# Two-layer hybrid encoder: attention bias made during the preceding feed-forward, layer norm vectors fetched later, eps added on VectorE, softmax normalising and transposes ordered later

## The chip, the cores and the metric

The kernel runs on one core of a Trainium2 chip. The metric is the device time of one execution in microseconds. The engines go by their names in the profile: PE is TensorE (PEld its weight loads), DVE is VectorE, ACT is ScalarE, POOL is GpSimd, SP is SyncE, which here issues every DMA of the kernel.

## The reference

An encoder of two layers over 256 tokens of 1024 features. Each layer is a feed-forward, three token mixers side by side, and a second feed-forward, each followed by a layer norm:

```python
for l in range(DEPTH):
    x = layer_norm(ALPHA * x + 0.5 * swiglu(x, ffn1_w_gate[l], ffn1_w_up[l], ffn1_w_down[l]), ln_g[l, 0], ln_b[l, 0])
    proj = x @ w_in[l]
    u, gb, gc, h, q, k, v = jnp.split(proj, splits, axis=-1)
    y_a = pool_mixer(u, pool_w[l], pool_scale[l])
    y_b = gated_conv_mixer(gb, gc, h, conv_w[l])
    y_c = neighbourhood_attention(q, k, v, rpb[l])
    y = jnp.concatenate([y_a, y_b, y_c], axis=-1) @ w_out[l]
    x = layer_norm(ALPHA * x + y, ln_g[l, 1], ln_b[l, 1])
    x = layer_norm(ALPHA * x + 0.5 * swiglu(x, ffn2_w_gate[l], ffn2_w_up[l], ffn2_w_down[l]), ln_g[l, 2], ln_b[l, 2])
```

`layer_norm` is `(x - mu) * rsqrt(var + eps) * g + b`; `swiglu` is `(silu(x @ w_gate) * (x @ w_up)) @ w_down` with an inner width of 2816. The attention has 8 heads of 64 features on a grid of 4 rows and 64 columns: a query sees 16 columns of all 4 rows, a learned bias that depends on the distance in rows and columns is added to its scores, scores outside its columns are set to -1e30, and a softmax follows.

## The kernel before

**Products and weights.** All 256 tokens stay on chip as two tiles of 128 (`t` = 0, 1), and all weights pass through once, in units of 512 KB. Products are to be exact in float32, so each weight unit is split into two parts: SP fetches it into `raw` (L183), ACT copies it to `whi`, rounded (L178), DVE subtracts that from `raw` into `wlo` (L179). Each activation is split the same way (`xhi`, `xlo`; L270 and L271), and each product is three matmuls: hi by hi, lo by hi, hi by lo. They stand in three helpers: `x_stat` (L290 to L292, one token tile against 512 columns), `w_stat` (L303 to L305, 128 columns against all tokens) and `r_stat` (L315 to L317, down and out projections). There are 4 `raw` buffers, so SP can be four units ahead of the splits, and 24 buffers for `whi` and `wlo`, so up to 12 units can be split and not yet used up.

**Order of the work.** Every engine runs its instructions in the order in which the code writes them. A `Pacer` sets it: each group of matmuls advances a clock of estimated TensorE time, `pc.at(delay, tag, fn)` writes a piece of work at the first step that is `delay` us later on this clock, `pc.need(tag)` writes it at once, and each step writes the load and split of one more unit, so long as no more than 12 are alive. The delays are constants at the top of the file. They place an instruction between others and hold nothing back at run time; there an instruction waits for its operands and for its buffers.

**Layer norm.** At the end of each part `finish` does the last products, and for each token tile `ln_stats` (L333, L334) and `ln_rest`: mean and variance are gathered (bn_aggr, L341), POOL adds eps (L342) and takes the power of -1/2 (L343) into `rs`, DVE subtracts the mean and multiplies by `lng` (L345, two halves), then multiplies by `rs` and adds `lnb` (L347, two halves). `transpose_x` then makes `xhi` and `xlo` of the next part: PE transposes (L268), ACT and DVE split (L270, L271). The vectors `lng` and `lnb` are copied to all 128 partitions by two DMAs of 512 KB each (`load_gb`, L325 and L326); `GB_AT` sets how long after the end of a part those of the next are fetched.

**Mixers.** For each token tile the projections `v` and `u` with one gate come first (`x_stat`); the second result is copied to `un` by ACT (L639) and transposed by PE (L644), and from it POOL makes the pooling mixer's means (L602 to L614), to which the pooling product (L619) belongs. Then `w_stat` makes q0, k0, q1, k1, and the two parts of the convolution mixer; the out projection and `finish` end the part.

**Attention.** Four heads are done after k0 (`q` = 0) and four after k1 (`q` = 1), in stages that are hooks of the Pacer: scores on PE (L686), bias added by DVE into `Sb` (L695), maximum (L697), exp on ACT into `pz` with its sum `sm` (L700); `A_NORM` later the normalising on DVE (reciprocal L710, multiplication L712); `A_TR` after that four transposes for each head on PE (L721), copied by ACT (L726, `PT`); `A_PV` after that the product with v (L735), split into `yT` by ACT and DVE (L748, L749).

**Bias.** `load_bias` (L568) fetches the bias of four heads by four DMAs on SP (L572) into `rbias`, and two additions on POOL (L579) put the mask on it, into `bias`. `rbias` and `bias` have one buffer each. For q = 0 this is written at the beginning of the mixers, which in POOL's order comes between the two powers of the layer norm and the means; for q = 1 it is written after the scores of q = 0.

**Feed-forward.** `ffn` does the first 512 of the 2816 columns with the token tiles apart (DVE's `hf`, L396, is transposed by PE, L408), then 9 pairs of 256 columns each for gate and up (`w_stat`), with the down projection (`r_stat`) of an earlier pair behind each; its loop is `for p in range(2, NPAIR)`.

Of the kernel before, what the change touches and what calls it, by code (L numbers as in the profile page):

```python
# [12 lines left out]
ALU = mybir.AluOpType  # L13
# [18 lines left out]
EPS = 1e-5  # L32
# [13 lines left out]

# units of the weights that go before the second token tile at the start, and where its transposes stand
X1_AT = 4
X1_TR = 3
# how long after its operands were ordered a step is issued, in microseconds of the tensor engine's work  # L50
LN_TR = (4.5, 7.2)
GB_AT = 14.0
H_TR = 4.1
# [3 lines left out]
A_STEP = 0.8  # L57
A_NORM = 2.6
A_TR = 1.2
A_PV = 1.4  # L60
# about how long a product of the tensor engine takes: these pace the work of the other engines
MM512 = 0.218
# [3 lines left out]
class Pacer:  # L66
    """Places work of the other engines, and the next weights, between groups of matrix products."""

# [52 lines left out]
def encoder_kernel(  # L121
# [34 lines left out]
    def mirrored(v):  # L156
        """The same view, its last axis run backwards."""
        dims = [list(d) for d in v.ap]
        step, n = dims[-1]
        dims[-1] = [-step, n]  # L160
        return bass.AP(tensor=v.tensor, offset=v.offset + (n - 1) * step, ap=dims)
# [7 lines left out]

# [1 line left out]
    def unit_tiles(shape):  # L171
# [33 lines left out]
    def behind(p):  # L205
        """The pairs whose down projection follows pair p's gate and up projections."""
        return [q for q in ([0, 1] if p == 2 else [p - 1]) if q < NPAIR - TAIL]
# [32 lines left out]

# [1 line left out]
    xs = [xp.tile([P, D], F32, tag=f"x{t}", name=nm("x")) for t in range(NT)]  # L242
# [29 lines left out]

# [1 line left out]
    def x_stat(ps, key, cols, t, xT, free):  # L274
        """One token tile against columns of the weights, a step per unit."""
        k = 1024 // cols
        ts = slice(t * P, (t + 1) * P)
        for i in range(KC // k):
            x_stat_unit(ps, key, i, cols, ts, xT)
            if free:  # L280
                pc.free((*key, i))
            if i < KC // k - 1:
                pc.step(3 * k * MM512)
# [10 lines left out]
    def w_stat(ps, key, xT):  # L294
        """256 columns of the weights against all tokens, transposed out."""
        for ft in range(2):
            c = slice(ft * P, (ft + 1) * P)
            for i in range(2):
                hi, lo = pc.get((*key, i))
                for j in range(4):  # L300
                    kc = i * 4 + j
                    o = ps[:, ft * SEQ : (ft + 1) * SEQ]
                    PE.matmul(o, hi[:, j, c], xT[0][:, kc, :], start=(kc == 0), stop=False)  # L303
                    PE.matmul(o, hi[:, j, c], xT[1][:, kc, :], start=False, stop=False)  # L304
                    PE.matmul(o, lo[:, j, c], xT[0][:, kc, :], start=False, stop=(kc == KC - 1))  # L305
                if ft == 1:
                    pc.free((*key, i))
                if ft == 0 or i == 0:
                    pc.step(12 * MM256)

    def r_stat(ps, key, act, t, n, first, last):
        """A chunk of transposed activations against half a row unit."""
        hi, lo = pc.get(key)
        ts = slice(t * P, (t + 1) * P)
        PE.matmul(ps, act[0][:, ts], hi[:, n, :], start=first, stop=False)  # L315
        PE.matmul(ps, act[1][:, ts], hi[:, n, :], start=False, stop=False)  # L316
        PE.matmul(ps, act[0][:, ts], lo[:, n, :], start=False, stop=last)  # L317

# [1 line left out]
    gbs = []  # L320
# [15 lines left out]
    def ln_rest(t, stats, store):  # L336
        g, b = gbs[-1]
        xt = xs[t]
        mv = sp.tile([P, 2], F32, tag="mv", name=nm("mv"))
        rs = sp.tile([P, 1], F32, tag="rs", name=nm("rs"))  # L340
        DVE.bn_aggr(mv, stats.rearrange("p a b -> p (a b)"))  # L341
        POOL.tensor_scalar(rs, mv[:, 1:2], EPS, None, ALU.add)  # L342
        POOL.tensor_tensor(rs, rs, half_t, ALU.pow)  # L343
        for h in range(2):
            DVE.scalar_tensor_tensor(xt[:, hs[h]], xt[:, hs[h]], mv[:, 0:1], g[:, hs[h]], ALU.subtract, ALU.mult)  # L345
        for c in hs:
            DVE.scalar_tensor_tensor(xt[:, c], xt[:, c], rs[:, 0:1], b[:, c], ALU.mult, ALU.add)  # L347
            if store:
                SP.dma_start(out[0, t * P : (t + 1) * P, c], xt[:, c])

    def finish(keys, act, acc, last_key, next_gb, store, stop):
        """The last products into acc, one token tile after the other, and the layer norm."""
        nT = None if store else new_xT()
        for t in range(NT):
            stats = sp.tile([P, 2, 6], F32, tag="stats", name=nm("stats"))
            # the first half of the columns is done early where something waits for the layer norm
            by_half = t == 0 or store
# [26 lines left out]

# [1 line left out]
    def new_h():  # L386
# [12 lines left out]
    def ffn(key, xT, next_gb, stop, store=False):  # L399
# [16 lines left out]

        # first four column tiles with the token tiles apart
        gk, uk = (*key, "g", 0), (*key, "u", 0)
# [42 lines left out]
        def act(k):  # L461
            f = k[-1]
            return [hts[f // 2][:, i, f % 2, :] for i in range(2)]

        for p in range(2, NPAIR):
            gate = bank()
            w_stat(gate, (*key, "g", p), xT)
            sg = silu(gate)
            pc.step(12 * MM256)
            up = bank()  # L470
            w_stat(up, (*key, "u", p), xT)
            hT = hts[p] = new_h()
            hf = gated(up, sg).rearrange("p (a b) -> p a b", a=2)
            ACT.copy(hT[:, 0], hf)  # L474
            DVE.tensor_tensor(hT[:, 1], hf, f32(hT[:, 0]), ALU.subtract)
            pc.step(12 * MM256)
            pc.need("h")
            # the down projection runs behind
            for q in behind(p):
                for f in (2 * q, 2 * q + 1):  # L480
                    k = (*key, "d", f)
                    for t in range(NT):
                        for n in range(2):
                            if acc[t][n] is None:
                                acc[t][n] = bank("acc")
                            r_stat(acc[t][n], k, act(k), t, n, f == 0, False)
                        if t == 1:
                            pc.free(k)
                        pc.step(6 * MM512)
        keys = [(*key, "d", f) for f in range(2 * (NPAIR - TAIL), NCH)]  # L490
        return finish(keys, act, acc, keys[-1], next_gb, store, stop)

# [1 line left out]
    consts = {}  # L494

    def setup():
        icnt = cp.tile([P, 2, SEQ], F32, tag="icnt", name="icnt")
        for g, w in enumerate(WINDOWS):
# [3 lines left out]
            for t in list(range(w // 2)) + list(range(SEQ - w // 2 + 1, SEQ)):  # L502
                cnt = min(t - w // 2 + w, SEQ) - max(t - w // 2, 0)
                POOL.memset(icnt[ps_ : ps_ + 64, j, t : t + 1], 1.0 / cnt)
        # additive mask of a query column block: its rows run with the column falling
        mask = cp.tile([P, 2, KW], F32, tag="mask", name="mask")
        POOL.memset(mask, 0.0)
        half = NA_COLS // 2
        for r in range(ROWS):
            for b in range(2):  # L510
                m = mask[r * QB : (r + 1) * QB, b, :]
                # key column minus query column is k + q + off
                off = b * KOFF - b * QB - (QB - 1)
# [30 lines left out]
        pc.at(30, "cw", columns)  # L544
        # the bias table, each line in the middle of a longer one
        tab = ap_.tile([P, 7 * TABW], F32, tag="a", name="tab")
# [7 lines left out]
        for r in range(ROWS):  # L554
            dt_ = tc.dram_tile([DEPTH * HEADS, ROWS, TABW], F32, name=f"tab{r}")
            pc.at(20 + 2 * r, "tab", lambda r=r, dt_=dt_: SP.dma_start(dt_, tabv[:, ROWS - 1 - r : 2 * ROWS - 1 - r, :]))
            tabs.append(dt_)
        # probabilities: the columns out of a block's reach stay zero
        pz = []
# [6 lines left out]

# [1 line left out]
    def load_bias(l, q):  # L568
        n = 4 * ROWS
        rv = bp.tile([P, n, WIN], F32, tag="rbias", name=nm("rbias"))  # L570
        for r in range(ROWS):
            SP.dma_start(  # L572
                rv[r * QB : (r + 1) * QB, :, :],
                dram(consts["tabs"][r], (l * HEADS + 4 * q) * ROWS * TABW, [[1, QB], [TABW, n], [1, WIN]]),
            )
        bias = bp.tile([P, 2, n, KW], F32, tag="bias", name=nm("bias"))
        for b in range(2):
# [4 lines left out]
            )  # L582
        return bias

    def mixers(l, xT, next_gb, stop):
# [11 lines left out]
        POOL.memset(U[:, :, PADL + SEQ :], 0.0)  # L597
        biases = {0: load_bias(l, 0)}

# [70 lines left out]
        def attention(j, qT, kT, q):  # L670
            """Two heads, in the upper and the lower half of the rows: one stage after the other."""
            st = {}
# [97 lines left out]
        qk(0)  # L770
        pc.at(A_S + A_STEP + 2, "bias1", lambda: biases.update({1: load_bias(l, 1)}))
        qk(1)
# [73 lines left out]
```

## Time and profile before

| | |
|---|---|
| runs before | 979.34, 980.66, 981.9 us; median 980.66 |
| span of the profiled execution (no other time is given for it) | 979.4 us |
| mean granted clock of TensorE | 0.991 |
| mixers of layer 0 and of layer 1, about | 198 to 296 us, 678 to 780 us |

The page cuts the span into 40 slices of 24.5 us. PE is below nine tenths busy in the first slice, in the tenth (220 to 245 us, in the mixers of layer 0), in the 29th and 30th (686 to 735, in those of layer 1), and in the last:

```profile
PE   7999999998999999999999999999889999999996
POOL 4000000024101000000000000002050000000001
PEclk9999999999999999999999999999989999999999
```

Each digit is the busy share of a slice in tenths; PEclk is the clock granted to PE, in tenths of full speed. POOL works at the start, where it makes constants, and in the mixers.

A row of a timeline is the start and the length in us, engine, line, operation and result<-operands, and in brackets the idle time ahead of it with what ended it. A row of the waits is who waited for what, with us in total, times, and the longest. SPq is the queue in which SP issues DMAs; its rows are the issue, not the transfer.

### The profile page before, as it was taken

Reading aid. Unit: us, or ns where it says so; the run is one execution under the profiler, and the core shown is the slowest. Engines: PE = TensorE matmul, PEld = TensorE weight load, DVE = VectorE, ACT = ScalarE, POOL = GpSimd, SP = SyncE. Lnnn points to the kernel's source line nnn. Section 1 sums busy time; section 2 is a strip of 40 time slices with the busy share of each in tenths; the row PEclk is TensorE's granted clock in tenths of the full one; section 3 lists DMA queues with packets and bytes.
Section 4 is the critical chain, followed back from the end, with each engine's and each line's share of the span. In section 5 each row is a group of like instructions: output and inputs, shape, how many; then the busy total and the mean of one; then the engine's idle time right before and its main releaser. Section 6 shows DMA issues by size and latency. Waiting matters only on the chain.

```text
span 979.4 us, 15259 instructions
## 1 busy us (share of the span) xinstructions
PE 950.6 (97%) x6201; PEld 865.1 (88%) x6201; DVE 580.3 (59%) x670; ACT 437.7 (45%) x585; POOL 65.6 (7%) x118
## 2 busy tenths in 40 slices
PE   7999999998999999999999999999889999999996
PEld 5999999878888999999888999998688889999995
DVE  5755544676768644545676454548676776454525
ACT  6544434335734534434344444443465354344410
POOL 4000000024101000000000000002050000000001
PEclk9999999999999999999999999999989999999999
DMA  8887665568345866565468556664754377556601
GB/s 287 277 264 216 190 194 173 145 185 241 106 129 169 258 194 188 175 195 177 135 211 254 176 172 194 191 186 110 252 153 123 109 229 243 177 174 193 192 23 43
DMA packets 129077, 178.95 MB, mean 183 GB/s; under 512 B 14752, under 2 KB 100848, under 8 KB 129008
## 3 DMA queue, kind: packets, MB, share of 16 engines
q1 hardware_dynamic: 129008, 177.99, 59.3%
q8 instruction: 48, 0.79, 0.3%
q14 instruction: 21, 0.17, 0.0%
HBM read 176.84 MB, written 1.13 MB: 182 GB/s over the span
## 4 chain that ended last, share of the span: by engine, by line
PE 83%; DVE 7%; DMA 5%; issue 2%; ACT 1%; POOL 1%; SPq 1%; POOLq 0%; DVEq 0%; ACTq 0%
PE mm L303 16%; PE mm L304 16%; PE mm L305 16%; PE acc L315 9%; PE acc L316 9%; PE acc L317 9%; DMA raw<-in_w_in_dram 3%; DVE wlo L179 2%; PE mm L292 2%; PE mm L290 2%; PE mm L291 2%; ACT whi L178 1%; PE mm L721 1%; DMA raw<-in_ffn_w_down_dram 1%; DMA raw<-in_ffn_w_up_dram 1%
## 5 line engine op out<-in xcount | busy, mean ns | idle before, releaser
L179 DVE TENSOR_TENSOR wlo<-raw,whi 128x1024 fp32r<-128x1024 f32 (+1 forms) x321 | 390.0, 1231 | 303.1 <-ACT whi L178 302.0
L178 ACT CAST whi<-raw 128x1024 fp32r<-128x1024 f32 (+1 forms) x321 | 331.1, 1045 | 328.9 <-issue 131.2
L303 PE MATMUL mm<-xhi,whi 128*128 128x256 f32 x1344 | 384.0, 286 | 0.0
L304 PE MATMUL mm<-xlo,whi 128*128 128x256 f32 x1344 | 382.0, 284 | 0.0
L305 PE MATMUL mm<-xhi,wlo 128*128 128x256 f32 x1344 | 381.8, 284 | 0.0
L303 PEld LDWEIGHTS mm<-xhi,whi 128*128 128x128 f32 x1344 | 259.7, 193 | 3.0 <-issue 1.5
L304 PEld LDWEIGHTS mm<-xlo,whi 128*128 128x128 f32 x1344 | 259.6, 193 | 1.4
L305 PEld LDWEIGHTS mm<-xhi,wlo 128*128 128x128 f32 x1344 | 259.5, 193 | 0.0
L315 PE MATMUL acc<-whi,hT 128*128 128x512 f32 x352 | 137.9, 392 | 0.0
L316 PE MATMUL acc<-whi,hT 128*128 128x512 f32 x352 | 137.4, 390 | 0.0
L317 PE MATMUL acc<-wlo,hT 128*128 128x512 f32 x352 | 137.0, 389 | 0.0
L317 PEld LDWEIGHTS acc<-wlo,hT 128*128 128x128 f32 x352 | 66.1, 188 | 14.0
L291 PE MATMUL mm<-whi,xlo 128*128 128x512 f32 x192 | 75.3, 392 | 2.9 <-DVE xlo L271 2.9
L315 PEld LDWEIGHTS acc<-whi,hT 128*128 128x128 f32 x352 | 66.2, 188 | 12.7
L316 PEld LDWEIGHTS acc<-whi,hT 128*128 128x128 f32 x352 | 66.2, 188 | 12.3
L290 PE MATMUL mm<-whi,xhi 128*128 128x512 f32 x192 | 76.7, 399 | 0.4 <-ACT whi L178 0.4
L292 PE MATMUL mm<-wlo,xhi 128*128 128x512 f32 x192 | 75.2, 392 | 0.5 <-DVE wlo L179 0.5
L342 POOL TENSOR_SCALAR rs<-mv 128x1 f32<-128x1 f32 x12 | 9.4, 780 | 847.0 <-DVE mv L341 847.0
L474 ACT CAST hT<-hf 128x512 fp32r<-128x512 f32 x36 | 22.3, 620 | 75.2 <-DVE hf L396 75.2
L291 PEld LDWEIGHTS mm<-whi,xlo 128*128 128x128 f32 x192 | 36.4, 189 | 10.8 <-DVE xlo L271 3.8
L292 PEld LDWEIGHTS mm<-wlo,xhi 128*128 128x128 f32 x192 | 36.2, 188 | 8.9 <-DVE wlo L179 1.3
L290 PEld LDWEIGHTS mm<-whi,xhi 128*128 128x128 f32 x192 | 36.3, 189 | 8.2 <-ACT whi L178 1.3
(93 smaller groups left out, 556.9 us busy)
## 6 DMA issues: line engine op xcount, KB each, us to landing
raw<-in_ffn_w_up_dram SPq DMA_DIRECT2D x88, 512.0 KB, 4.7
raw<-in_ffn_w_down_dram SPq DMA_DIRECT2D x88, 512.0 KB, 4.1
raw<-in_ffn_w_gate_dram SPq DMA_DIRECT2D x87, 512.0 KB, 4.1
raw<-in_w_in_dram SPq DMA_DIRECT2D x40, 512.0 KB, 4.7
raw<-in_w_out_dram SPq DMA_DIRECT2D x16, 512.0 KB, 4.8
lng<-in_ln_g_dram SPq DMA_DIRECT2D x6, 512.0 KB, 6.8
lnb<-in_ln_b_dram SPq DMA_DIRECT2D x6, 512.0 KB, 8.3
rbias<-tab SPq DMA_DIRECT2D x16, 96.0 KB, 5.1
```

Of the source, the lines that this page charges most:

```text
L178: ACT.copy(hi, raw)
L179: DVE.tensor_tensor(lo, raw, f32(hi), ALU.subtract)
L290: PE.matmul(ps, xT[0][:, kc, ts], hi[:, j, :], start=(kc == 0), stop=False)
L291: PE.matmul(ps, xT[1][:, kc, ts], hi[:, j, :], start=False, stop=False)
L292: PE.matmul(ps, xT[0][:, kc, ts], lo[:, j, :], start=False, stop=(kc == KC - 1))
L303: PE.matmul(o, hi[:, j, c], xT[0][:, kc, :], start=(kc == 0), stop=False)
L304: PE.matmul(o, hi[:, j, c], xT[1][:, kc, :], start=False, stop=False)
L305: PE.matmul(o, lo[:, j, c], xT[0][:, kc, :], start=False, stop=(kc == KC - 1))
L315: PE.matmul(ps, act[0][:, ts], hi[:, n, :], start=first, stop=False)
L316: PE.matmul(ps, act[1][:, ts], hi[:, n, :], start=False, stop=False)
L317: PE.matmul(ps, act[0][:, ts], lo[:, n, :], start=False, stop=last)
L474: ACT.copy(hT[:, 0], hf)
```

## The change

Five things change. The eps addition goes from POOL to DVE (new L343). `GB_AT` goes from 14 to 45. `A_NORM` goes from 2.6 to 3.6 and `A_TR` from 1.2 to 2.2, so that the normalising is written 1 us later on the Pacer's clock, and the transposes and the products with v 2 us later. `load_bias` is cut into `fetch_bias` (the DMAs, new L579) and `add_mask` (the additions, new L590): for q = 0 both, and for q = 1 the fetch, are written in the first feed-forward of the layer, at the pair p = 6. The additions for q = 1 stay in the mixers, 1 us later on the clock than before. Comments and docstrings go too. Line numbers rise by 1 up to about line 462 and by 7 to 13 behind it: L721 becomes L734, L712 becomes L725.

```diff
@@
-GB_AT = 14.0
+GB_AT = 45.0
...
-A_NORM = 2.6
-A_TR = 1.2
+A_NORM = 3.6
+A_TR = 2.2
 A_PV = 1.4
+BIAS_AT = A_S + A_STEP + 3.0
@@ ln_rest
         DVE.bn_aggr(mv, stats.rearrange("p a b -> p (a b)"))
-        POOL.tensor_scalar(rs, mv[:, 1:2], EPS, None, ALU.add)
+        DVE.tensor_scalar(rs, mv[:, 1:2], EPS, None, ALU.add)
         POOL.tensor_tensor(rs, rs, half_t, ALU.pow)
@@ ffn
+        def bias_ahead():
+            ahead["bias"] = {0: add_mask(fetch_bias(key[0], 0))}
+            ahead["rv"] = fetch_bias(key[0], 1)
+
         for p in range(2, NPAIR):
+            if key[1] == 0 and p == 6:
+                pc.at(0, "bias", bias_ahead)
@@
-    def load_bias(l, q):
+    def fetch_bias(l, q):
         n = 4 * ROWS
         rv = bp.tile([P, n, WIN], F32, tag="rbias", name=nm("rbias"))
...
+        return rv
+
+    def add_mask(rv):
+        n = 4 * ROWS
         bias = bp.tile([P, 2, n, KW], F32, tag="bias", name=nm("bias"))
...
         return bias
 
+    ahead = {}
+
@@ mixers
-        biases = {0: load_bias(l, 0)}
+        biases, rv1 = dict(ahead.pop("bias")), ahead.pop("rv")
...
         qk(0)
-        pc.at(A_S + A_STEP + 2, "bias1", lambda: biases.update({1: load_bias(l, 1)}))
+        pc.at(BIAS_AT, "bias1", lambda: biases.update({1: add_mask(rv1)}))
         qk(1)
```

SP's order in the mixers of layer 0, before: the layer norm vectors stand among the weights of the k0 and q1 projections (`in_w_in_dram`).

```order
L183 DMA raw_2206<-in_w_in_dram 128x4x256
L183 DMA raw_2218<-in_w_in_dram 128x4x256
L325 DMA lng_2230<-in_ln_g_dram 128x1024
L326 DMA lnb_2231<-in_ln_b_dram 128x1024
L183 DMA raw_2234<-in_w_in_dram 128x4x256
L183 DMA raw_2247<-in_w_in_dram 128x4x256
L183 DMA raw_2260<-in_w_in_dram 128x4x256
```

SP's order at pair 6 of the first feed-forward now, where before the two down units were followed directly by the two gate units:

```order
L184 DMA raw_1183<-in_ffn_w_down_dram 128x1024
L184 DMA raw_1201<-in_ffn_w_down_dram 128x1024
L579 DMA rbias_1220<-tab_588 32x16x48
L579 DMA rbias_1220<-tab_589 32x16x48
L579 DMA rbias_1220<-tab_590 32x16x48
L579 DMA rbias_1220<-tab_591 32x16x48
L579 DMA rbias_1228<-tab_588 32x16x48
L579 DMA rbias_1228<-tab_589 32x16x48
L579 DMA rbias_1228<-tab_590 32x16x48
L579 DMA rbias_1228<-tab_591 32x16x48
L184 DMA raw_1257<-in_ffn_w_gate_dram 128x4x256
L184 DMA raw_1277<-in_ffn_w_gate_dram 128x4x256
```

The eight bias fetches moved here from the mixers; the second four write the buffer that the first four filled. In the mixers, SP's rows around the layer norm vectors are now these, behind the last units of the out projection:

```order
L184 DMA raw_2649<-in_w_out_dram 128x1024
L184 DMA raw_2688<-in_w_out_dram 128x1024
L326 DMA lng_2771<-in_ln_g_dram 128x1024
L327 DMA lnb_2772<-in_ln_b_dram 128x1024
L184 DMA raw_2775<-in_ffn_w_gate_dram 128x2x512
L184 DMA raw_2807<-in_ffn_w_gate_dram 128x2x512
```

The vectors moved past 14 weight units.

DVE's order in the attention of layer 0, q = 0, from the last maximum on, before:

```order
L695 TENSOR_TENSOR Sb_2499<-acc_2487,bias_2098 128x320
L697 TENSOR_REDUCE mx_2501<-Sb_2499 128x2
L710 RECIPROCAL sm_2476<-sm_2476 128x2
L712 TENSOR_SCALAR pz_592<-pz_592,sm_2476 128x4x40 x2
L710 RECIPROCAL sm_2483<-sm_2483 128x2
L712 TENSOR_SCALAR pz_594<-pz_594,sm_2483 128x4x40 x2
```

And now:

```order
L708 TENSOR_TENSOR Sb_2500<-acc_2488,bias_1225 128x320
L710 TENSOR_REDUCE mx_2502<-Sb_2500 128x2
L180 TENSOR_TENSOR wlo_2533<-raw_2531,whi_2532 128x1024
L723 RECIPROCAL sm_2477<-sm_2477 128x2
L725 TENSOR_SCALAR pz_592<-pz_592,sm_2477 128x4x40 x2
L723 RECIPROCAL sm_2484<-sm_2484 128x2
L725 TENSOR_SCALAR pz_594<-pz_594,sm_2484 128x4x40 x2
```

A split of a weight (`wlo`) moved ahead of the normalising.

PE's order around the transposes of the same heads, before (between the projections q1, `mm_2453`, and k1, `mm_2607`):

```order
L303 MATMUL mm_2453<-xhi_1960,whi_2219 128x256
L304 MATMUL mm_2453<-xlo_1961,whi_2219 128x256
L305 MATMUL mm_2453<-xhi_1960,wlo_2220 128x256
L721 MATMUL mm_2573<-ident,pz_592 128x128 x4
L721 MATMUL mm_2580<-ident,pz_594 128x128 x4
L721 MATMUL mm_2587<-ident,pz_596 128x128 x4
L721 MATMUL mm_2594<-ident,pz_598 128x128 x4
```

And now (`mm_2572` is the projection k1, `pT` the pooling mixer's means):

```order
L304 MATMUL mm_2572<-xhi_1973,whi_2249 128x256
L305 MATMUL mm_2572<-xlo_1974,whi_2249 128x256
L306 MATMUL mm_2572<-xhi_1973,wlo_2250 128x256
L632 MATMUL mm_2600<-pT_2332,pw 128x256 x2
L734 MATMUL mm_2609<-ident,pz_592 128x128 x4
L734 MATMUL mm_2616<-ident,pz_594 128x128 x4
L734 MATMUL mm_2623<-ident,pz_596 128x128 x4
L734 MATMUL mm_2630<-ident,pz_598 128x128 x4
L304 MATMUL mm_2572<-xhi_1973,whi_2236 128x256
```

The transposes moved 24 matmuls on, into the middle of k1, and behind the pooling product, which stood behind the product with v before.

## Prediction

> **What bounds the kernel now.** I read the page's share of each engine first, then TensorE's waits, then, at the lines named there, the windows, the timelines and the chain.
>
> ```profile
> PE 950.6 (97%) x6201; PEld 865.1 (88%) x6201; DVE 580.3 (59%) x670; ACT 437.7 (45%) x585; POOL 65.6 (7%) x118
> ...
> 95.00:178.00 83.00, 83.00 (x608) 79.17 (x608) 42.89 (x40) 35.79 (x41) 0.00 (x0) 1.00 0.61 181
> ```
> The second row is a window of steady feed-forward (length; busy time of PE, PEld, DVE, ACT, POOL; granted clock; DMA share; GB/s): PE is busy for all of its 83.00 us, so nothing of the change can gain there. All that can go is in what PE waits for:
>
> ```profile
> PE mm L644 <- ACT un L639: 6.2, 2, 3.2
> PE mm L268 <- DMA x<-in_x_dram: 4.8, 2, 3.6
> PE mm L721 <- DVE pz L712: 4.6, 4, 1.4
> PE mm L291 <- DVE xlo L271: 2.9, 2, 1.5
> PE mm L408 <- DVE hf L396: 1.1, 2, 0.9
> ```
> (us in total, times, longest.) L268 is the load of x at the start, which the change leaves alone. The other four come in pairs or fours, once or twice per layer: 14.8 us.
>
> **Layer norm in front of the mixers (L291), gain 2.9.**
>
> ```profile
> 192.71 1.42 DVE L347 SCALAR_TENSOR_TENSOR x<-x,rs,lnb 128x512 f32<-128x512 f32 x2 [0.46 <-POOL rs L343]
> ...
> 202.43 4.10 DVE L347 SCALAR_TENSOR_TENSOR x<-x,rs,lnb 128x512 f32<-128x512 f32 x2 [0.47 <-POOL rs L343]
> ...
> 202.46 3.52 POOL L579 TENSOR_TENSOR bias<-rbias,mask 128x640 f32<-128x640 f32 x2
> ...
> 209.65 0.39 PE L292 MATMUL mm<-wlo,xhi 128*128 128x512 f32 x1
> 209.88 0.39 PE L290 MATMUL mm<-whi,xhi 128*128 128x512 f32 x1
> 211.73 0.50 PE L291 MATMUL mm<-whi,xlo 128*128 128x512 f32 x1 [1.47 <-DVE xlo L271]
> ```
> The same pair of L347 takes 1.42 us for the first token tile and 4.10 for the second, where the two bias additions run on POOL: 2.68 longer. The Trainium skill ("SBUF — State Buffer", SBUF: two separate sides) calls the port that VectorE and GpSimd share an exclusive lock, held for a whole instruction; the 4.10 against 1.42 agrees. In the changed kernel no addition stands there, so DVE comes to xlo some 2.7 us earlier, and PE's 1.47 us of waiting ends, in both layers: 2.9. Behind a wait PE also restarts slowly: from 209.88 to 211.73 are 1.85, of which 1.47 is wait and 0.23 one product (209.65 to 209.88); 0.15 is left, which goes with each wait.
>
> **Fetch of the layer norm vectors (L644 and L408), gain 9.0 and 1.1.**
>
> ```profile
> 209.80 0.42 SPq L326 DMA_DIRECT2D lnb<-in_ln_b_dram  x1
> ...
> 210.32 9.67 DMA raw<-in_w_in_dram
> ...
> raw<-in_w_in_dram SPq DMA_DIRECT2D x40, 512.0 KB, 4.7
> ...
> 227.76 1.11 PE L644 MATMUL mm<-ident,un 128*128 128x128 f32 x4 [3.17 <-ACT un L639]
> ...
> 498.47 9.60 DMA raw<-in_ffn_w_down_dram
> ```
> The chain runs through a weight transfer of 9.67 us, issued at 210.32, right behind lnb (and lng ahead of it, 0.5 MB each), where the median of its kind is 4.7: some 5 late, and the split of that weight (and un behind it on ACT) is late at PE, which stands 3.17 at L644. At the start of the next feed-forward the chain has the same (9.60), and L408 stands. Moved to 45 us, lng and lnb fall behind the weights of the out projection, into stretches where weights wait for free buffers (rows of SP below). Removed: 6.2 and 1.1. The long wait costs the clock too:
>
> ```profile
> 223.00:228.50 5.50, 2.33 (x17) 2.12 (x16) 4.56 (x4) 3.89 (x5) 0.00 (x0) 0.90 0.86 267
> 228.50:231.00 2.50, 2.50 (x14) 2.50 (x13) 1.56 (x2) 1.06 (x2) 1.30 (x1) 0.53 0.83 293
> ```
> Around and behind it the granted clock is 0.90 and 0.53: PE's busy time there is longer by 2.33 x 0.10 + 2.50 x 0.47 = 1.4, in both layers 2.8. So 6.2 + 2.8 = 9.0. Unknown is the new price of lng and lnb: from nothing, if weights are far enough ahead, to the two 3.17 us and their clock again, if they aren't; I take nothing, since these places have no wait of PE in the steady row.
>
> **Attention, net gain 2.9.** Before, the normalising (L712) is in DVE's order right behind the maxima, and PE's transposes (L721) wait for it (rows of DVE, POOL, ACT and PE in layer 0, one timeline after the other):
>
> ```profile
> 246.71 2.67 DVE L712 TENSOR_SCALAR pz<-pz,sm 128x160 f32<-128x160 f32 x2
> 249.30 0.15 DVE L710 RECIPROCAL sm<-sm 128x2 f32<-128x2 f32 x1
> 249.48 0.52 DVE L712 TENSOR_SCALAR pz<-pz,sm 128x160 f32<-128x160 f32 x2
> ...
> 251.16 1.22 DVE L179 TENSOR_TENSOR wlo<-raw,whi 128x1024 fp32r<-128x1024 f32 x1
> ...
> 246.16 3.05 POOL L579 TENSOR_TENSOR bias<-rbias,mask 128x640 f32<-128x640 f32 x2 [5.45 <-DVE Sb L695]
> ...
> 248.53 1.03 ACT L178 CAST whi<-raw 128x1024 fp32r<-128x1024 f32 x1
> ...
> 247.96 0.30 PE L721 MATMUL mm<-ident,pz 128*128 128x128 f32 x1 [0.87 <-DVE pz L712]
> ...
> 251.60 0.36 PE L303 MATMUL mm<-xhi,whi 128*128 128x256 f32 x1
> ...
> 254.64 1.95 PE L735 MATMUL mm<-PT,v 128*64 128x256 f32 x16
> 256.52 1.13 PE L619 MATMUL mm<-pT,pw 128*128 128x256 f32 x4
> ...
> 267.58 2.55 PE L721 MATMUL mm<-ident,pz 128*128 128x128 f32 x16
> ```
> The first normalising takes 2.67 beside POOL's second additions instead of 0.52. These begin when the last Sb has been read, and no table moves that. But the order puts a split (wlo) ahead of the normalising now, and it waits for whi, which ACT makes behind the eight exps: 248.53 + 1.03 = 249.56. Then wlo 1.22, the reciprocal and the first pair of L712 (0.15 + 0.52): the first pz is there at about 251.5. POOL is done by 249.2, so its cover is gone. PE was ready at 247.96 - 0.87 = 247.1. Ahead of the transposes it has now the 24 products that stood behind them (251.60 to 254.64: 3.0) and the pooling product (at most 1.13): ready between 250.1 and 251.2. It waits 0.3 to 1.4; I take 1.0, where layer 0 waited 2.0 (11.00 less 8.95 in the window below). In the second half, which had no wait (267.58), the same 24 products bring PE to 270.6, and whi, wlo and the first pair follow the exps:
>
> ```profile
> 267.90 1.03 ACT L178 CAST whi<-raw 128x1024 fp32r<-128x1024 f32 x1
> ```
> 267.90 + 1.03 + 1.22 + 0.67 = 270.8, and the weighted products of the first half and their yT now stand right ahead of these scores on DVE, some 0.9 (an estimate: a wlo of 1.22 less what it overlaps), so 271.7: a wait of about 1.2. New: 2 x (1.0 + 1.2) = 4.4, about as much as goes (4.6); I count the two as even. Its bounds are 0 and, if whi comes late in each, 2 x 3.2.
>
> What goes besides is clock. The three windows are attention in layer 0, and twice in layer 1:
>
> ```profile
> 241.00:252.00 11.00, 8.95 (x74) 7.76 (x73) 10.72 (x23) 8.41 (x27) 3.13 (x4) 1.00 0.40 134
> ...
> 722.00:734.00 12.00, 9.43 (x66) 8.89 (x65) 10.71 (x22) 8.28 (x26) 3.57 (x5) 0.80 0.32 100
> 734.00:737.50 3.50, 3.50 (x24) 3.37 (x23) 1.23 (x1) 1.12 (x2) 0.00 (x0) 0.71 0.55 153
> ```
> Two microseconds idle in 11 left the clock at 1.00; 2.6 in 12 took it to 0.80 and 0.71: 9.43 x 0.20 + 3.50 x 0.29 = 2.9. With about 1.0 in each stretch I expect no drop: gain 2.9.
>
> **Cost at nothing, with its cover.** In the feed-forward ahead of the mixers SP now issues four small transfers, and four more that need the same single buffer:
>
> ```profile
> 178.42 2.06 SPq L572 DMA_DIRECT2D rbias<-tab  x4
> ...
> DMA to landing us min/median/max: 4.6/5.1/6.3
> ...
> L579 POOL TENSOR_TENSOR bias<-rbias,mask x8: 1540/1550/2013, 202.5 to 728.3; 128x640 f32<-128x640 f32 x8
> ...
> SPq L183 <- DVE wlo L179: 71.1, 29, 4.0
> ```
> The second four wait until both additions have read the first: 2.06 + 5.1 + 2 x 1.55 + 2.06 = 12.3 us in which no weight is asked for. In the steady window SP waits 71.1 of 83 us for a free buffer, 29 times: a unit lasts 83 / 29 = 2.9 us, four are landed or in flight and up to 12 split, so I put the reserve at 30 us and the cost at nothing; without the reserve it is 12.3 per layer. The additions can hold up one wlo there by 3.1 us, inside the same reserve. The two transfers of lng and lnb are in the same position.
>
> The eps addition leaves POOL for DVE, six layer norms with two tiles each. DVE has no such row; the nearest is its reciprocal of a column pair, 0.15 (above), and the other end is nothing, since DVE idles 0.46 ahead of L347 anyway.
>
> ```profile
> 200.60 0.78 POOL L342 TENSOR_SCALAR rs<-mv 128x1 f32<-128x1 f32 x1 [7.92 <-DVE mv L341]
> ```
> 0.78 becomes some 0.15 to 0.2, so L347 waits little or no more; it counts at the end of the program alone, where nothing covers it: 0.3. Elsewhere it is hidden by the products of the next stage.
>
> **The sum**, against the profiled span of 979.4: 2.9 (L291) + 9.0 (L644 with its clock) + 2.9 (attention's clock, its waits even) + 1.1 (L408) + 0.3 (end) + 4 x 0.15 = 0.6 (restarts of the two L291 and two L408) = 16.8, so 962.6. The page gives no other time for that execution; the runs' median of 980.66 is 1.3 above the span, which I add: **963.9 us**. If the two least certain terms, attention's new waits and the clock behind them, miss by 3 either way, it is 961 to 967.
>
> **The rivals.**
> 1. *Attention's new waits cost the clock.* The first wait stands behind whi, so it can be 2 or 3 instead of 1. For it: 2.6 us in two pieces was enough in layer 1. Against: 2.0 was not, in layer 0. Price: 2.9 in each layer, where the sum has none: 963.9 + 5.8 = 969.7. By the Trainium skill ("TensorE: Matmul & The Clock Gate", What's actually happening) the clock halves after an idle window of about 3.4 us, which runs freely; by that, waits near 1 would cost nothing, and the 0.80 after 2.6 in pieces shows that less is enough.
> 2. *The waits vanish*, because whi is earlier on ACT with L644 undelayed: 963.9 - 4.4 = 959.5. Against it: whi stands behind the exps in the order.
> 3. *L644 stays.* It is the ring of four raw buffers that makes weights late there, not lng and lnb: 963.9 + 9.0 = 972.9. Against it: 9.67 against a median of 4.7.
> 4. *Slower: the 12.3 us of SP starve PE* in both first feed-forwards, with a drop of the clock behind each (1.2 as 2.50 x 0.47): 963.9 + 2 x 13.5 = 990.9. It decides where fewer than five units (12.3 / 2.9) are in reserve; SP's 71.1 us of waiting for buffers speak against it.
> 5. *The change doesn't do what it says:* the time of POOL's additions comes back beside other DVE work and all waits find new causes: 980.7.
>
> **How the numbers follow.** Chances: forecast 0.51, rival 1 0.20, rival 2 0.12, rival 3 0.10, rival 4 0.04, rival 5 0.03. The range takes the forecast's own, rival 2 with 3 below it, and rival 1 with 2 above: 956.5 to 971.5; rivals 3 to 5 (0.17) are left out. Faster by over 0.3% (what a measurement of this kernel can tell from no change) is all but rivals 4 and 5: 0.93; within 0.3%: 0.03; slower: 0.04.
>
> **What would show it.** Right: L644, L291 and L408 gone from PE's waits; L347 at 1.42 in both tiles; no raw transfer near 9.6 in the mixers; L734 (the transposes' new line) with four waits of about 1; clock 1.00 in both layers' mixers. Wrong: a wait of PE on whi or wlo in a first feed-forward (rival 4), L644 in the list (rival 3), a clock under 0.9 behind the transposes (rival 1). The weakest step is the 1.0 and 1.2 of attention, which rest on ACT's order and not on a row.

## The result and the profile after

The changed kernel takes 966.28 us (median of 4 runs, 964.41 to 966.65), the kernel before in the same comparison 981.28 (979.34 to 982.71): a ratio of 0.9848, with a 95% interval of 0.9832 to 0.9865. The gain is 15.0 us where 16.8 was forecast. The profiled execution has a span of 964.9 against 979.4. The page and then TensorE's waits of the changed kernel:

```profile
PE 946.9 (98%) x6201; PEld 861.3 (89%) x6201; DVE 572.1 (59%) x682; ACT 437.4 (45%) x585; POOL 58.6 (6%) x106
...
PE   7999999998999999999999999999999999999996
```

```profile
PE mm L269 <- DMA x<-in_x_dram: 4.9, 2, 3.5
PE mm L657 <- ACT un L652: 3.4, 2, 2.5
PE mm L734 <- DVE pz L725: 1.4, 4, 0.6
PE mm L409 <- DVE hf L397: 0.3, 1, 0.3
```

L269 is the start, which stayed. L291's wait on xlo (L292 now) has left the list. L657 is the old L644: 3.4 us are left of 6.2. L734 is the old L721: 1.4 of 4.6. L409 is the old L408: 0.3 of 1.1. Of the three slices that showed the mixers before, one still has an 8: the tenth, in layer 0, where L657 waits 2.47 us. The windows (columns as in the prediction) say what the clock did:

```profile
95.00:178.00 83.00, 83.00 (x608) 79.17 (x608) 43.10 (x40) 35.75 (x41) 4.33 (x2) 1.00 0.66 190
225.00:229.00 4.00, 3.77 (x20) 3.78 (x21) 2.50 (x3) 1.45 (x3) 2.33 (x2) 0.61 0.78 219
240.00:256.00 16.00, 15.68 (x125) 13.64 (x121) 10.66 (x26) 12.69 (x34) 3.16 (x4) 1.00 0.62 197
712.00:728.00 16.00, 15.45 (x128) 13.81 (x126) 12.19 (x25) 12.30 (x33) 3.63 (x5) 1.00 0.60 198
```

The first row is the feed-forward that now carries the bias: PE is busy for all of its 83.00 us. The second is behind the wait at L657 in layer 0: the clock falls to 0.61, which costs 3.77 x 0.39 = 1.5 us. Both attentions run at 1.00.

So the trace's 14.5 us are: L291 2.9; L657 6.2 - 3.4 = 2.8, and its clock 2.8 - 1.5 = 1.3; attention's waits 4.6 - 1.4 = 3.2 and its clock 2.9; L409 0.8; restarts and end 0.8 (an estimate: the rows from the gathering of the variance to L348 take 1.64 us at the end instead of 2.12, and each of two restarts is put at 0.15). Together 14.7.

**What is still late at L657.** The chain ahead of it in layer 0, and ACT and DVE in the stretch before (timelines):

```profile
214.57 2.13 DVE wlo L180 x2
216.70 0.02 issue
216.72 6.83 DMA raw<-in_w_in_dram
...
223.64 1.04 ACT whi L179
224.69 0.49 ACT un L652
225.18 0.04 issue
225.22 0.66 PE mm L657 x4
```

```profile
209.99 0.59 ACT L652 COPY un<-mm 128x512 f32<-128x512 f32 x1 [2.10 <-PE mm L293]
211.79 0.37 ACT L658 COPY U<-mm 128x256 f32<-128x256 f32 x1 [1.21 <-PE mm L657]
...
212.19 0.42 DVE L659 COPY GB<-mm 128x256 f32<-128x256 f32 x1 [3.11 <-ACT U L658]
```

The product that ACT copies to `un` is done at 221.3; the copy stands on ACT behind a split whose weight lands at 223.5, and starts at 224.6. That weight was asked for at 216.72, when a split freed one of the four raw buffers. Ahead of that, ACT and DVE, which run in order, stood still for the first tile: ACT 2.10 for un and 1.21 for U, DVE 3.11 for GB. The DMA engines were busy for 0.18 of the time from 212 to 216 us and for 0.93 from 216 to 224. That these standstills make the splits, and so the weights, late is read from the order; no run tests it by itself. The forecast had made lng and lnb the cause. The experiments take the wait apart.

### The profile page after: what moved, and what is told of

Read it like the earlier page. It is cut to its first block, busy times and chain, and to the rows that moved or that the text cites. A ratio compares the mean times of both kernels' runs of the same rounds, so it can differ in the third digit from the quotient of the medians.

```text
span 964.9 us, 15250 instructions
## 1 busy us (share of the span) xinstructions
PE 946.9 (98%) x6201; PEld 861.3 (89%) x6201; DVE 572.1 (59%) x682; ACT 437.4 (45%) x585; POOL 58.6 (6%) x106
## 3 DMA queue, kind: packets, MB, share of 16 engines
HBM read 176.84 MB, written 1.13 MB: 184 GB/s over the span
## 4 chain that ended last, share of the span: by engine, by line
PE 89%; ACT 3%; DVE 3%; DMA 3%; issue 1%; SPq 0%; DVEq 0%; ACTq 0%
PE mm L304 15%; PE mm L305 15%; PE mm L306 15%; PE acc L316 10%; PE acc L317 10%; PE acc L318 10%; PE mm L293 4%; PE mm L291 4%; PE mm L292 4%; DVE wlo L180 2%; ACT whi L179 2%; ACT pz L713 1%; DMA raw<-in_w_in_dram 1%; PE mm L734 1%; DMA raw<-in_ffn_w_up_dram 1%; PE mm L269 1%
## 5 line engine op out<-in xcount | busy, mean ns | idle before, releaser
L291 PE MATMUL mm<-whi,xhi 128*128 128x512 f32 x192 | 77.0, 401 | 0.0
L292 PE MATMUL mm<-whi,xlo 128*128 128x512 f32 x192 | 75.4, 393 | 0.0
L344 POOL TENSOR_TENSOR rs<-rs,half_t 128x1 f32<-128x1 f32 x12 | 11.7, 977 | 653.4 <-DVE rs L343 653.4
L291 PEld LDWEIGHTS mm<-whi,xhi 128*128 128x128 f32 x192 | 36.4, 190 | 8.1 <-ACT whi L179 1.2
L292 PEld LDWEIGHTS mm<-whi,xlo 128*128 128x128 f32 x192 | 36.5, 190 | 7.1
```

The costliest lines, as they stand in the source:

```text
L291: PE.matmul(ps, xT[0][:, kc, ts], hi[:, j, :], start=(kc == 0), stop=False)
L292: PE.matmul(ps, xT[1][:, kc, ts], hi[:, j, :], start=False, stop=False)
```

## The experiments

All times are medians; each ratio is to the kernel before, run on the same chip beside it. The changed kernel's 966.28 is from a comparison of its own. Of two kernels whose intervals overlap, the waits in the trace decide, not the times.

### The wait at L657 (L644): fetch, ring of raw buffers, order

**e1_gb14**, the changed kernel with one number put back:

```diff
-GB_AT = 45.0
+GB_AT = 14.0
```

> The changed kernel with GB_AT back at 14. If the 1 MB of lng and lnb is what makes the weights late ahead of L657, its waits go from 3.4 us back to about 6.2, its clock loss from 1.5 to 2.8, and L409's waits from 0.3 to 1.1: some 4.9 us longer, about 971. If the four raw buffers and the order of ACT and DVE make them late, whatever else SP fetches, L657 stays near 3.4 and the time within 1 us of 966.3.

968.04 us; 0.9875 (0.9844 to 0.9906). Its waits:

```profile
PE mm L657 <- ACT un L652: 4.5, 2, 2.4
```

Neither theory's number: 4.5 lies between 3.4 and 6.2. The weight behind lnb took 9.27 us again in its chain, against 6.83, but the wait is only 1.1 us longer. Even that is not clear of chance: in e2, e4, e7 and e9, which leave this stretch as it is in the changed kernel, the same wait is 2.5 to 3.1 us.

**e8_before_gb45**, the same number in the kernel before, alone:

```diff
-GB_AT = 14.0
+GB_AT = 45.0
```

> The kernel before with GB_AT 45 and nothing else. If the fetch of lng and lnb alone makes the wait at L644, its 6.2 us fall to about 0, with 2.8 of clock and 1.1 at L408: 10 us shorter, about 971. If it is one cause among others (with it back in the changed kernel the wait was 4.5 instead of 3.4), about 1 to 3 us of the wait go: 976 to 979.

973.66 us; 0.9943 (0.9920 to 0.9967), 6.0 us shorter.

```profile
PE mm L644 <- ACT un L639: 2.8, 2, 1.7
```

In the kernel before, the fetch makes 6.2 - 2.8 = 3.4 us of the wait, beside L408's 1.1, which is gone from the list, and the clock behind it, which stays at 1.00 in both layers. The other 2.8 at L644 (1.69 in layer 0, 1.13 in layer 1) stay, with lng and lnb far away: another cause.

**e12_before_u_tr** leaves lng and lnb where they were and moves only the place at which PE needs un:

```diff
-U_TR = 2.6
-POOL_AT = 16.0
+U_TR = 5.2
+POOL_AT = 13.4
```

> The kernel before with U_TR 5.2 and POOL_AT 13.4 and nothing else, so lng and lnb still stand among the weights. If only un is late there, 2.7 to 2.9 us of products in front of L644 hide most of its 6.2 us, and the clock stays at 1.00 behind it: some 8 us shorter, about 972. If the weights themselves are late by 5 us behind lng and lnb, PE waits at L303 or L305 instead, and the time stays near 980.

973.48 us; 0.9941 (0.9915 to 0.9966).

```profile
PE mm L721 <- DVE pz L712: 5.5, 5, 1.6
...
PE mm L644 <- ACT un L639: 0.7, 1, 0.7
```

L644 falls from 6.2 to 0.7 and no wait on a weight takes its place: even with the late fetch, PE didn't lack weights in this stretch, it lacked un. The median falls by 6.2 where 8 was expected, and the profiled span by 7.7; the waits in the attention rise by 0.9, with the clock behind them at 0.58 and 0.57 in the two layers.

**e5_u_tr**, the same edit in the changed kernel:

> The changed kernel with the transposes of un (L657) ordered 2.6 us of products later (U_TR 5.2, POOL_AT 13.4, which leaves the pooling product where it is). If what is left at L657 is un standing on ACT behind a split whose weight lands late, PE has products for those 2.5 us: no wait at L657, clock 1.00 behind it, about 961.5. If all weights are late there and not only the one ahead of un, PE waits at the products (L304 or L306) instead: 965 to 967.

962.80 us; 0.9820 (0.9796 to 0.9845). L657 has left the list; behind the start it begins with:

```profile
PE mm L734 <- DVE pz L725: 1.5, 4, 0.8
PE mm L409 <- DVE hf L397: 0.6, 3, 0.2
```

**e6_raw5** gives the changed kernel one raw buffer more and one split unit less (22 buffers are 11 units):

```diff
-W_SLOTS = 24
-RAW_SLOTS = 4
+W_SLOTS = 22
+RAW_SLOTS = 5
```

> The changed kernel with five raw buffers and 22 buffers of split weights (11 units) in place of four and 24. If the ring of four raw buffers makes the weight ahead of un late, one more lets SP ask one unit earlier, and L657's waits of 3.4 us shrink below 1.5: 962 to 964. If it is ACT and DVE, which split nothing while un and U wait for PE, the fifth buffer changes the waits by less than 1 us: about 966, or more with one unit less in reserve.

963.05 us; 0.9822 (0.9798 to 0.9846).

```profile
PE mm L657 <- ACT un L652: 0.5, 1, 0.5
```

The wait falls as the first theory said, but not for its reason: the edit has two numbers, and the second one moves un. With 11 split units instead of 12, each split is written one place later, and un of the second tile stands behind 85 splits on ACT where it stood behind 86 (245 and 246 in layer 1). Three of SP's requests for weights of the projections, in the changed kernel, and then the same requests here with the chain to un:

```profile
214.40 2.69 SPq L184 DMA_DIRECT2D raw<-in_w_in_dram  x3
```

```profile
216.09 2.69 SPq L184 DMA_DIRECT2D raw<-in_w_in_dram  x3
...
217.22 6.08 DMA raw<-in_w_in_dram
...
223.40 1.05 ACT whi L179
224.45 0.49 ACT un L652
```

From the first transposes in front of the mixers (193.70 and 195.39) to these requests it is 20.70 us in both: with both numbers changed, SP asks no earlier. In the changed kernel un stands behind the third of these weights (216.72, in the chain above), here behind the second, which lands no earlier than it did there (27.9 us after those transposes, against 27.0). So it is un's place on ACT that takes 2.9 of the 3.4 us. What a fifth raw buffer alone would do, and so whether the ring of four makes these weights late, as rival 3 has it, no run shows.

### The order in the attention

**e2_order_back**, the changed kernel with both numbers of the attention put back:

```diff
-A_NORM = 3.6
-A_TR = 2.2
+A_NORM = 2.6
+A_TR = 1.2
```

> The changed kernel with A_NORM 2.6 and A_TR 1.2 as before. If the place of normalising and transposes made those waits, L734 waits 4.6 us again instead of 1.4, and the clock in layer 1's attention falls to about 0.8 again: 3.2 + 2.9, about 972.4. If that clock came from the long wait at L644 and not from the attention's own waits, the waits return and the clock stays at 1.00: about 969.5. If both were late because of late weights, neither returns: 966.3.

969.55 us; 0.9889 (0.9857 to 0.9922). L734 waits 4.9 us in four pieces, as before the change. The windows of layer 0 and layer 1, and below them the same stretch of layer 0 in e8, which has the same order:

```profile
240.00:252.00 12.00, 9.65 (x66) 8.95 (x65) 9.95 (x23) 9.45 (x27) 3.13 (x4) 0.86 0.56 184
...
715.00:727.00 12.00, 9.43 (x64) 9.07 (x65) 9.92 (x22) 8.28 (x27) 3.13 (x4) 0.86 0.52 176
```

```profile
240.00:252.00 12.00, 9.66 (x81) 8.60 (x78) 10.68 (x22) 9.41 (x27) 3.53 (x5) 1.00 0.56 189
```

The waits return, and the clock with them: 0.86 in both layers, a loss of (9.65 + 9.43) x 0.14 = 2.7. So the attention's own waits take the clock down, without the long wait ahead of it: L657's longest is 1.4 here, and the clock behind it 1.00. But not each time: e8 idled as long in layer 0 and kept 1.00. The time is that of the second theory (969.5), which the windows refute; it is 2.9 below the first one's since L657 waits 2.5 here instead of 3.4 and its clock loss of 1.5 is gone.

**e7_norm26_tr32** takes the split that now stands ahead of the normalising away from there, and leaves PE's order:

```diff
-A_NORM = 3.6
-A_TR = 2.2
+A_NORM = 2.6
+A_TR = 3.2
```

> The changed kernel with A_NORM 2.6 and A_TR 3.2: the normalising stands ahead of the weight split on DVE again, and PE's transposes stay where the change put them. If the split ahead of the normalising makes the 1.4 us that L734 still waits, they go: about 964.7. If POOL's additions (L590) hold the first L725 for some 2.7 us, as before, the first pz is still there before PE (3.9 us of other work stand ahead), so no wait either; a wait of over 0.5 would need another cause.

963.79 us; 0.9835 (0.9809 to 0.9860).

```profile
PE mm L657 <- ACT un L652: 3.0, 2, 1.5
...
PE mm L734 <- ACT PT L739: 1.0, 2, 0.5
PE mm L734 <- ACT ya L636: 0.8, 1, 0.8
```

The waits on pz are gone, though the first L725 took 2.71 us beside POOL's additions. New ones are there, which the expectation didn't have: PE waits for ACT's ya and PT, which the transposes don't read. In the code the results of the projections, of the pooling product and of the transposes share four banks of PSUM, the memory that PE writes to, so a bank that ACT has not yet copied out can hold a transpose up. e11 tests that for ya; for PT it is read from the code.

**e10_u_tr_norm** is e5 and e7 together:

> Both together (U_TR 5.2, POOL_AT 13.4, A_NORM 2.6, A_TR 3.2). If the two waits are separate, their gains add: no wait at L657 and L734, about 960. If one hides behind the other, as much as the better of the two alone.

961.01 us; 0.9805 (0.9777 to 0.9832). L657 and the waits on pz are both gone, 1.5 us on ya and PT are left: the gains are separate.

**e11_pool16** is e10 with the pooling product behind the product with v again (its lines are against e10):

```diff
-POOL_AT = 13.4
+POOL_AT = 16.0
```

> The last combination (U_TR 5.2, A_NORM 2.6, A_TR 3.2) with POOL_AT at 16 again, so that the pooling product stands behind the product with v. If the third head's transposes waited on ACT's ya only because the pooling product held a PSUM bank, that wait (0.5 us) goes: about 960.5. If PE now comes to the transposes 1 us earlier than pz is there, it waits on L725 instead: 961.

958.74 us (958.20 to 959.71); 0.9790 (0.9764 to 0.9816), an interval below that of the changed kernel. PE's waits behind the start, the first four:

```profile
PE mm L734 <- ACT PT L739: 0.5, 1, 0.5
PE mm L293 <- DVE wlo L180: 0.4, 1, 0.4
PE acc L317 <- DVE hT L414: 0.3, 1, 0.3
PE mm L409 <- DVE hf L397: 0.2, 1, 0.2
```

The wait on ya is gone, as expected, and none on pz came. This has the lowest median of the study (its interval and that of e10 overlap): the changed kernel with three other numbers (U_TR 5.2, A_NORM 2.6, A_TR 3.2).

### The bias and the eps

**e3_bias_back** makes the bias in the mixers again:

```diff
-            if key[1] == 0 and p == 6:
-                pc.at(0, "bias", bias_ahead)
...
-        biases, rv1 = dict(ahead.pop("bias")), ahead.pop("rv")
+        biases = {0: add_mask(fetch_bias(l, 0))}
...
-        pc.at(BIAS_AT, "bias1", lambda: biases.update({1: add_mask(rv1)}))
+        pc.at(BIAS_AT, "bias1", lambda: biases.update({1: add_mask(fetch_bias(l, 1))}))
```

> The changed kernel with fetch and additions of the bias back in the mixers, at the places of before (for q = 1 at BIAS_AT). If POOL's additions beside L348 delay xlo, L348 takes about 4.1 us at the second token tile again and PE waits 1.47 at L292 in each layer, with restarts 3.2 us: about 969.5, or up to 1.5 more if L657 comes later too. If the place of the bias has no effect on PE: 966.3.

969.05 us; 0.9881 (0.9851 to 0.9912). The second tile's L348 of layer 0 in this kernel, then in the changed one, and the wait that follows here:

```profile
201.82 4.02 DVE L348 SCALAR_TENSOR_TENSOR x<-x,rs,lnb 128x512 f32<-128x512 f32 x2
...
PE mm L292 <- DVE xlo L272: 1.9, 2, 1.0
```

```profile
201.94 1.41 DVE L348 SCALAR_TENSOR_TENSOR x<-x,rs,lnb 128x512 f32<-128x512 f32 x2
```

4.02 against 1.41 with only the bias moved: the additions on POOL hold DVE up. PE then waits 0.97 in each layer and not 1.47; the difference fits the 0.46 for which DVE no longer idles ahead of L348, as POOL doesn't add eps.

**e9_bias4x** stretches the time in which SP asks for no weight, by making the bias of q = 0 four times:

```diff
-            ahead["bias"] = {0: add_mask(fetch_bias(key[0], 0))}
+            for _ in range(4):
+                ahead["bias"] = {0: add_mask(fetch_bias(key[0], 0))}
```

> The changed kernel with the fetch and additions for q = 0 made four times over, one after the other, in each first feed-forward. SP, which asked for no weight for 13.8 us in the changed kernel, then asks for none for about 13.8 + 3 x 9.3 = 42 us. If the reserve of split weights is 30 us, PE waits about 12 us there in each layer, with a drop of the clock behind each: about 992. If the reserve were only a little over 13.8, PE would wait 25 us or more in each: over 1016. If no wait shows, the reserve is over 42: 966.

994.43 us (2 runs); 1.0153 (1.0108 to 1.0199). SP's queue in the changed kernel, with ACT at that place, and then the same of this kernel with PE's wait:

```profile
98.95 13.80 SPq L579 DMA_DIRECT2D rbias<-tab  x8
...
117.47 1.05 ACT L179 CAST whi<-raw 128x1024 fp32r<-128x1024 f32 x1 [9.63 <-DMA raw<-in_ffn_w_gate_dram]
```

```profile
98.69 36.68 SPq L580 DMA_DIRECT2D rbias<-tab  x20
...
139.84 1.04 ACT L179 CAST whi<-raw 128x1024 fp32r<-128x1024 f32 x1 [32.27 <-DMA raw<-in_ffn_w_gate_dram]
...
PE acc L316 <- ACT hT L482: 23.0, 2, 11.6
```

In the changed kernel SP is held for 13.80 us and ACT's splits for 9.63, and PE loses nothing. Held for 36.68, PE waits 11.6 and 11.4: the reserve is about 36.7 - 11.6 = 25 us, with 30 estimated. What ends first isn't the weights that PE reads: PE waits for hT, which ACT makes from hf, and hf stands on DVE behind the `wlo` of a weight that isn't there yet, much as un did on ACT.

**e4_eps_pool** undoes the move of the eps:

```diff
-        DVE.tensor_scalar(rs, mv[:, 1:2], EPS, None, ALU.add)
+        POOL.tensor_scalar(rs, mv[:, 1:2], EPS, None, ALU.add)
```

> The changed kernel with the eps addition back on POOL. If only the last layer norm is uncovered, the end is 0.4 us longer and the rest the same: 966.7. If each of the twelve tiles counts, 12 x 0.46 = 5.5 longer: 971.8.

967.50 us; 0.9861 (0.9817 to 0.9906): too wide to place 0.4 us. In the trace DVE idles 0.46 ahead of L348 in all twelve tiles again. PE's waits are those of the changed kernel but for L657 (3.0) and a wait of 1.0 for a weight in the first 11 us, so no layer norm but the last shows in them: the trace fits the first theory, with 0.46 at the end of the program.

## Why the prediction was right, and where it was off

The forecast was 963.9 with a range of 956.5 to 971.5; 966.28 lies in it, and the direction and the places were right. That the total came so close is in part luck: L644 gave 4.9 less than forecast and the attention 3.2 more. By its own terms:

- **L291, 2.9:** as forecast. e3 shows the cause by itself, 4.02 against 1.41.
- **L644 with its clock, 9.0: mis-sized, 4.1 came.** The step that failed is "Removed: 6.2 and 1.1": it read one late transfer in the chain as the whole cause of the wait. The runs showed a second cause. With the fetch moved and nothing else, 2.8 us stay at L644 (e8): 3.17 become 1.69 in layer 0, and 3.05 become 1.13 in layer 1. What stays is the place of un on ACT, behind a split whose weight isn't there yet. The wait goes when PE needs un later, with the fetch late or not (e12, e5), and falls to 0.5 when un stands one split earlier (e6). The chain shows one path; the next one was 1.5 to 1.9 us behind it. By the prediction's own sign (L644 in the list) rival 3 came true for this part; that the ring of raw buffers is what makes those weights late is seen in the chain (a request at 216.72, as a buffer comes free) and was not tested by itself. "I take nothing", the price of lng and lnb in their new place, held: PE has no new wait there.
- **Attention, 2.9: mis-sized the other way, 6.1 came.** The clock's 2.9 came as forecast, and e2 took 2.7 of it back. The step that was mis-sized is the new waits, set at 4.4 and measured 1.4. In the first half the mechanism was right: the split ends, the first pz follows, and PE waits for it.

```profile
246.96 1.23 DVE L180 TENSOR_TENSOR wlo<-raw,whi 128x1024 fp32r<-128x1024 f32 x1 [3.00 <-ACT whi L179]
...
248.30 0.52 DVE L725 TENSOR_SCALAR pz<-pz,sm 128x160 f32<-128x160 f32 x2
...
248.75 2.55 PE L734 MATMUL mm<-ident,pz 128*128 128x128 f32 x16 [0.32 <-DVE pz L725]
266.58 2.54 PE L734 MATMUL mm<-ident,pz 128*128 128x128 f32 x16 [0.26 <-DVE pz L725]
```

  The bounds had been 0.3 to 1.4, and 0.32 (0.55 in layer 1) is the low end: the pooling product covers its full time. In the second half the 0.9 us by which the scores were to come later didn't show; without it the same sum gives 0.2, and 0.26 was measured. Rival 1 (clock lost behind these waits) didn't come, with waits of 0.55 at most. Two sums of the prediction are off by a little: its rows give 1.1 for the second wait and not 1.2, and 971.7 for the top of the range and not 971.5.
- **L408, 1.1:** 0.8 came, 0.3 is left. **End, 0.3:** 0.5 came; L348 follows L346 with no idle time.
- **SP, at nothing:** right. 13.80 and 12.64 us measured against 12.3, covered in both layers; e9 puts the cover at 25 and not 30. Rival 4 would have needed nearly twice the standstill.

## What to carry to other kernels

A chain names the path that came last; before its whole wait is booked as a gain, look how late the next path is, and test with one change that moves the need (e12) and one that removes the cause (e8). Where an engine runs in order, a result that is ready can stand behind a weight that isn't: move the use later (e5), or the copy one place ahead (e6), before making the transfers faster. When a number such as a count of buffers also sets the order of the work, read the order in the trace before crediting the buffers. A reserve that hides a standstill has a size, and stretching the standstill once measures it.

## What the runs showed of the hardware that I hadn't expected

- The granted clock can fall behind waits that are short, and doesn't each time. One wait of 2.47 us was followed by 0.61 (changed kernel). In one execution of e8, two waits of together 2.34 us at the same place of the program were followed by 1.00 in layer 0 and by 0.57 in layer 1; in e2, 2.35 us in layer 0 by 0.86. The Trainium skill ("TensorE: Matmul & The Clock Gate", What's actually happening) says that the clock halves after an idle window of about 3.4 us, and that this window runs freely. A wait of 2.47 us is shorter than it, and the measurement decides; that like waits drop the clock once and not another time fits a window that isn't tied to the program.
- The first 14 us differ by 2 us from one execution to the next. PE comes to the transposes in front of the mixers for the second time at 206.18 in the changed kernel and at 208.29 in e1, though both have the same instructions up to there (L269 in the timelines of PE). The second token tile's first transposes come at 13.64 in the one and at 15.73 in the other: the difference is there already. Ahead of them, products of 512 columns follow each other 0.41 us or more apart until 11.2 us in the changed kernel and until 15.5 in e1, and 0.23 apart soon behind that, while the granted clock reads 1.00 in both. Spans that differ by 2 us say nothing until the start is taken off. The kernel before (13.61) and the changed kernel start alike.
